# Three of four merge-gate pairs in a Strassen form, interleaved with the branch products of a hybrid decoder layer

## Chip, cores and metric

The kernel runs on one core of one Trainium2 chip. The metric is the device time of one execution in microseconds: 1034.13 us is the median of three runs (1033.95 to 1034.41). TensorE (PE) multiplies, VectorE (DVE) and ScalarE (ACT) work elementwise, GpSimd (POOL) issues some of the transfers, and SyncE (SP) issues the weight loads.

## The reference

One decoder layer for 256 tokens and 2048 channels, all in float32. Its last part is what the change is about:

```python
h = rmsnorm(x, pre_norm_g)
proj = h @ w_in      # ..., g_mla, g_conv (2048 x 2048 each)
attn = causal_mla(...) * silu(z_mla)
y_mla = attn @ w_o_mla
y_conv = (b_gate * conv(c_gate * c_in) * silu(z_conv)) @ w_o_conv
merged = sigmoid(g_mla) * y_mla + sigmoid(g_conv) * y_conv
x = x + rmsnorm(merged @ w_out, post_norm_g)
```

The two merge gates are products of the normed input with 2048 x 2048 weights; so are the two branch outputs and the output projection, each with its own operand.

## The kernel before

**Split products.** Every float32 operand is split into a high part, rounded by ScalarE (`split_act`, L245, `whi`), and the rest, subtracted by VectorE (L246, `wlo`). A product takes three matmuls: high by high, high by low, low by high (`product`). TensorE keeps the order of the program (`matmul`, L88); the other engines run in an order that a scheduler writes when the kernel is built, and each engine works through its own list in that order.

**Units.** Weights come in units of 128 x 2048 float32 (1 MB): four blocks of the contraction by 512 output columns. A unit is loaded by SyncE into one of three `raw` buffers, and split in two halves of 1024 columns, each into one of five `whi` and one of five `wlo` buffers. `ahead` loads three units ahead and splits one ahead of the unit that `take` hands to TensorE. With 256 tokens (two tiles `t` of 128) a unit feeds 2 x 4 x 3 = 24 matmuls of 512 columns: for each token tile the first half, then the second.

**The end of the layer.** After the 16 heads (`at_f` holds the attention branch, `cv_f` the convolution branch) come four column chunks `c` of 512. In each, `tokens(c, n, cols)` makes four blocks: n=0 and n=1 are the two gates (from `x_both`), n=2 the attention branch (`at_both`), n=3 the convolution branch (`cv_both`). A block is four units, 96 matmuls into two PSUM banks named `sq`. Sigmoids by ScalarE make `sg`, VectorE multiplies and adds, the merged chunk is turned through DRAM by GpSimd (`turned`) and split into `m_both` (`features`) while the next chunk's first block runs. In chunk 0 the splits of the branches stand between the units of the first blocks. At the end stands the output projection, `out`.

Unit numbers appear in names: `wlo113` to `wlo116` are the units of block (0, 0), `117` to `120` of block (0, 1).

Of the kernel before, what the change touches and what calls it, by code (L numbers as in the profile page):

```python
# [82 lines left out]
def tile_layer(ctx: ExitStack, tc: tile.TileContext, xw, w0, xb, x, pos, pvec, post_g, wc, wz, wcv, wkr, wqk, wqr, wv, cwr, wsq, out):  # L83
# [55 lines left out]
    u_d = [[[add(wsq[n, c, k]) for k in range(4)] for n in range(4)] for c in range(4)]  # L139
# [28 lines left out]
    def split_unit(i):  # L168
# [22 lines left out]
        for h in range(0, w, HALF):  # L191
            n = min(HALF, w - h)
            if u_out[3, 0] <= i < u_out[3, 3]:
                hi, lo = (op.tile([P, HALF], F32R, name=f"w{o}{i}_{h}") for o in ("hi", "lo"))
# [18 lines left out]
    def take(i):  # L213
        ahead(i)
        parts = splits.pop(i)
# [11 lines left out]
    def product(ps, a, b, first, last):  # L227

        (ah, al), (bh, bl) = a, b
        matmul(ps, ah, bh, start=first, stop=False)  # L230
        matmul(ps, ah, bl, start=False, stop=False)
        matmul(ps, al, bh, start=False, stop=last)
# [51 lines left out]
    hp = main.enter_context(tc.tile_pool(name="hp", bufs=1))  # L284
    x_both = hp.tile([P, KD, 2 * S], F32R, name="x_both")
    fstack = main.enter_context(ExitStack())
# [3 lines left out]
    bstack = main.enter_context(ExitStack())  # L290
# [394 lines left out]
    def values(h, pt):  # L685
# [15 lines left out]
        nc.vector.tensor_tensor(at, f[:, :].rearrange("p (t i x) -> p t i x", t=NT, i=4), at, op=ALU.mult)  # L701


    at_t = at_f[:, :, :].rearrange("p (v t k) s -> p v t (k s)", v=NV, t=NT)
    z_ps = {}
# [56 lines left out]
    def channels_join(j, t):  # L762
# [4 lines left out]
        go, come = turned(u, via, 4)  # L767
        go()
        return lambda: come(u)
# [151 lines left out]
    cp = main.enter_context(tc.tile_pool(name="cp", bufs=1))  # L921
    at_both = cp.tile([P, H, 2 * S], F32R, name="at_both")
    cv_both = cp.tile([P, KD, 2 * S], F32R, name="cv_both")
    dp = main.enter_context(tc.tile_pool(name="dp", bufs=1))

    def split_turned(src, both, c, t):
        ks, ts = slice(4 * c, 4 * c + 4), slice(t * P, (t + 1) * P)
        lo = slice(t * P + S, (t + 1) * P + S)
        split_act(quarters(both[:, ks, ts]), quarters(both[:, ks, lo]), by_rows(src, 4), True)

    def split_branch(i):

        for t in range(NT):
            split_turned(at_t[:, i, t, :], at_both, i, t)

    def split_channels(i):

        j, t = divmod(i, NT)
        split_turned(cv_t[:, j, t, :], cv_both, j, t)

    def tokens(c, n, cols):

        pss = [bank(f"sq{c}_{n}_{t}") for t in range(NT)]
        for kk in range(4):
            w = take(u_d[c][n][kk])
            if c == 0 and n == 0:
                split_branch(kk)
            if c == 0 and n in (1, 2):
                split_channels(4 * (n - 1) + kk)
            for t in range(NT):  # L950
                for k4 in range(4):
                    k = 4 * kk + k4
                    a = [cols[:, k, o + t * P : o + (t + 1) * P] for o in (0, S)]
                    product(pss[t][:, :], a, w(k4, 512), k == 0, k == KD - 1)
        return pss

    def wide(name, t, bufs=1):
        return dp.tile([P, 512], F32, name=f"{name}{t}", tag=f"{name}{t}", bufs=bufs)

    def features(c, m, m_both):  # L960

        for t in range(NT):
            split_turned(m[t][:, :], m_both, c, t)

    make_identity(nc, ident[:, :])
    waiting = m_both = None
    for c in range(4):
        gates = []
        for n in range(2):
# [224 lines left out]
```

## Time and profile before

| | |
|---|---|
| median of three runs (range) | 1034.13 us (1033.95 to 1034.41) |
| span of the profiled execution, first to last instruction | 1032.9 us |
| mean granted TensorE clock | 0.999 |
| chain that ended last | TensorE 99% |
| HBM read, written | 215.66 MB, 12.58 MB |

The profiled execution has no time of its own beside its span; the three runs lie 1.1 to 1.5 us above the span. In the groups, a line has the source line, the engine, the operation, what it writes and reads, shape and count, then busy time and mean duration, then the idle time ahead of it and what ended it. In the timeline, a line begins with start and duration in us, and a wait ahead of the row stands in brackets at its end. A line number may be that of a helper (L88 is every matmul), so one reads by the names of tiles.

### The profile page before, as it was taken

Reading aid. Unit: us, or ns where it says so; the run is one execution under the profiler, and the core shown is the slowest. Engines: PE = TensorE matmul, PEld = TensorE weight load, DVE = VectorE, ACT = ScalarE, POOL = GpSimd, SP = SyncE. Lnnn points to the kernel's source line nnn. Section 1 sums busy time; section 2 is a strip of 40 time slices with the busy share of each in tenths; the row PEclk is TensorE's granted clock in tenths of the full one; section 3 lists DMA queues with packets and bytes.
Section 4 is the critical chain, followed back from the end, with each engine's and each line's share of the span. In section 5 each row is a group of like instructions: output and inputs, shape, how many; then the busy total and the mean of one; then the engine's idle time right before and its main releaser. Section 6 shows DMA issues by size and latency. Waiting matters only on the chain.

```text
span 1032.9 us, 12670 instructions
## 1 busy us (share of the span) xinstructions
PE 1026.4 (99%) x4648; PEld 854.6 (83%) x4648; DVE 687.9 (67%) x973; ACT 531.3 (51%) x750; POOL 174.2 (17%) x324
## 2 busy tenths in 40 slices
PE   9999999999999999999999999999999999999997
PEld 8888888888888888888888888888888888888886
DVE  7588777787687777777777785564455455455562
ACT  7675555655456464564555465344434444443551
POOL 4620421104210223112133120020010001002000
PEclk9999999999999999999999999999999999999999
DMA  9775766558675676857676765565565556558642
GB/s 356 280 257 214 269 215 227 207 191 297 212 252 193 209 279 210 278 184 242 229 271 222 267 217 200 204 222 188 201 218 208 188 202 243 183 187 335 231 165 81
DMA packets 44669, 233.24 MB, mean 226 GB/s; under 512 B 7968, under 2 KB 10656, under 8 KB 21696
## 3 DMA queue, kind: packets, MB, share of 16 engines
q1 hardware_dynamic: 32544, 199.67, 54.4%
q0 software_dynamic: 11632, 29.48, 8.9%
q10 hardware_dynamic: 432, 3.29, 0.8%
q8 instruction: 36, 0.59, 0.2%
q14 instruction: 25, 0.20, 0.1%
HBM read 215.66 MB, written 12.58 MB: 221 GB/s over the span
## 4 chain that ended last, share of the span: by engine, by line
PE 99%; DVE 0%; ACT 0%; issue 0%
PE cv L88 34%; PE sq L88 34%; PE z L88 8%; PE out L88 8%; PE qa L88 2%; PE kn L88 2%; PE qn L88 2%; PE vv L88 2%; PE ckv L88 2%; PE qr L88 1%; PE o L88 1%; PE sw L88 1%; PE sc L88 1%; PE idle L88 0%; PE kr L88 0%; DVE og L1048 0%
## 5 line engine op out<-in xcount | busy, mean ns | idle before, releaser
L246 DVE TENSOR_TENSOR wlo<-raw,whi 128x1024 fp32r<-128x1024 f32 (+1 forms) x370 | 440.5, 1196 | 276.6 <-ACT whi L245 265.5
L245 ACT ACTIVATE whi<-raw 128x1024 fp32r<-128x1024 f32 (+1 forms) x372 | 382.7, 1035 | 412.2 <-PE sq L88 180.5
L88 PE MATMUL cv<-whi,x_both 128*128 128x512 f32 x1024 | 319.8, 389 | 0.0
L88 PEld LDWEIGHTS cv<-whi,x_both 128*128 128x128 f32 x1024 | 192.3, 188 | 39.6
L88 PE MATMUL cv<-wlo,x_both 128*128 128x512 f32 x512 | 199.4, 390 | 0.0
L88 PE MATMUL sq<-whi,x_both 128*128 128x512 f32 x512 | 158.2, 389 | 0.0
L88 PEld LDWEIGHTS sq<-whi,x_both 128*128 128x128 f32 x512 | 96.1, 188 | 19.8
L88 PEld LDWEIGHTS cv<-wlo,x_both 128*128 128x128 f32 x512 | 96.1, 188 | 19.3
L88 PE MATMUL sq<-wlo,x_both 128*128 128x512 f32 x256 | 99.6, 389 | 0.0
L88 PE MATMUL z<-whi,x_both 128*128 128x512 f32 x256 | 80.0, 389 | 0.0
L88 PE MATMUL sq<-whi,at_both 128*128 128x512 f32 x256 | 79.4, 389 | 0.0
L88 PE MATMUL sq<-whi,cv_both 128*128 128x512 f32 x256 | 79.4, 389 | 0.0
L88 PE MATMUL out<-whi,m_both 128*128 128x512 f32 x256 | 79.0, 389 | 0.0
L328 POOL DMA_DIRECT2D far<-sg x32 | 17.5, 553 | 305.8 <-DVE sg L320 232.6
L328 POOL DMA_DIRECT2D far<-via x64 | 35.2, 557 | 191.4 <-DVE via L320 190.0
L88 PEld LDWEIGHTS sq<-wlo,x_both 128*128 128x128 f32 x256 | 48.1, 188 | 10.0
L88 PEld LDWEIGHTS out<-whi,m_both 128*128 128x128 f32 x256 | 48.1, 188 | 10.0
L88 PEld LDWEIGHTS sq<-whi,cv_both 128*128 128x128 f32 x256 | 48.1, 188 | 9.9
L88 PEld LDWEIGHTS sq<-whi,at_both 128*128 128x128 f32 x256 | 48.1, 188 | 9.9
L88 PEld LDWEIGHTS z<-whi,x_both 128*128 128x128 f32 x256 | 48.1, 188 | 9.9
L88 PE MATMUL z<-wlo,x_both 128*128 128x512 f32 x128 | 49.8, 389 | 0.0
L88 PE MATMUL sq<-wlo,at_both 128*128 128x512 f32 x128 | 49.8, 389 | 0.0
(227 smaller groups left out, 1131.3 us busy)
## 6 DMA issues: line engine op xcount, KB each, us to landing
raw<-wsq_dram SPq DMA_DIRECT2D x80, 1024.0 KB, 4.8
raw<-wcv_dram SPq DMA_DIRECT2D x64, 1024.0 KB, 5.5
raw<-wz_dram SPq DMA_DIRECT2D x16, 1024.0 KB, 4.8
raw<-wqk_dram SPq DMA_DIRECT2D x8, 1024.0 KB, 6.1
cw<-cwr_dram POOLq DMA_DIRECT2D x24, 256.0 KB, 5.8
raw<-wc_dram SPq DMA_DIRECT2D x4, 1024.0 KB, 9.8
raw<-wv_dram SPq DMA_DIRECT2D x4, 1024.0 KB, 5.3
far<-via POOLq DMA_DIRECT2D x64, 48.0 KB, 4.1
```

What stands on the lines that cost most here:

```text
L88: return tc.keep_in_program_order(nc.tensor.matmul(*a, **kw))
L245: a = nc.scalar.activation(hi, src, AF.Copy)
L246: b = nc.vector.tensor_tensor(lo, src, hi.bitcast(F32), op=ALU.subtract)
L328: tc.keep_in_program_order(queue.dma_start(out=f[i], in_=m))
```

## The change

Chunk 0 keeps its two plain gate blocks. For chunks 1, 2 and 3 the gate pair is taken as one product of a 2 x 2 block matrix: rows are the two token tiles, columns the two halves of the contraction on the input's side, and the two gates on the weights' side. It is formed with seven products of 128 tokens by 1024 contraction by 512 columns, in the order Q1, V5, V6, V7, V4, V3, Q2, accumulated in three PSUM banks (`sX`, `sZ`, `sY`). A product has two units; a unit feeds 12 matmuls. The seven sums of the input (`form_11` to `form_3`) are made once, beside the gate blocks of chunk 0, from a second copy of x (`xf`). The weight sums are made for each chunk by VectorE in place (`nc.vector.tensor_tensor` on 128 x 2048, L1152 of the new file): V5, V6, V7 and V4 have two each. In names, `slo1_V51_0` is the low part of chunk 1, product V5, unit 1, half 0; `b1_0_2` is the raw unit 2 of gate 0 in chunk 1.

The products of a pair are interleaved with the units of two branch blocks: chunk 1's pair with the attention blocks 0 and 1, chunk 2's with 2 and 3, chunk 3's with the convolution blocks 0 and 1; the convolution blocks 2 and 3 stand by themselves. `at_both` and `cv_both` now share four tiles in the place of `x_both`. The attention and convolution branches, the gates and the half merged chunks are written to DRAM and read back (`keep`, `again`, `turned_unit`). Loads run four units ahead, splits two. The space for descriptors of GpSimd's transfers is set to 4096 bytes.

```diff
-    u_d = [[[add(wsq[n, c, k]) for k in range(4)] for n in range(4)] for c in range(4)]
+    u_d = [[[None] * 4 for n in range(4)] for c in range(4)]
+    for n, c in [(0, 0), (1, 0)] + [(n, c) for n in (2, 3) for c in range(4)]:
+        for k in range(4):
+            u_d[c][n][k] = add(wsq[n, c, k])
...
-        go, come = turned(u, via, 4)
+        go, _ = turned(u, via, 4, far_cv[j][:, 512 * t : 512 * (t + 1)])
         go()
-        return lambda: come(u)
+        return lambda: None
...
+    def keep(key, t):
+        kept[key] = dram.tile([P, 512], F32, name="kept_" + "_".join(map(str, key)))
+        tc.keep_in_program_order(nc.gpsimd.dma_start(out=kept[key][:, :], in_=t[:, :]))
+
+    def again(key, t):
+        tc.keep_in_program_order(nc.gpsimd.dma_start(out=t[:, :], in_=kept[key][:, :]))
...
+    def make_forms():
...
+        for i, h in enumerate(halves):
+            for k in range(KH):
+                nc.vector.scalar_tensor_tensor(
+                    h[:, k, :], h[:, k, :], col("pre_g", KH * i + k), r_x[:, :], op0=ALU.mult, op1=ALU.mult
+                )
+            yield
...
+        form_split("11", a11)
+        u, w, f3, f7 = sums
...
+    def branch_block(c, both):
...
+            early()
+            for t in range(NT):
+                nc.vector.tensor_tensor(y[t][:, :], pss[t][:, :], y[t][:, :], op=ALU.mult)
+                keep(("m", c, t), y[t])
...
+    def paired(c):
...
+        def split(name, src, plus):
+            def go():
+                t = raw[src]
+                if plus:
+                    nc.vector.tensor_tensor(t[:, :], t[:, :], raw[plus][:, :], op=ALU.add)
+                out = []
+                for h in range(2):
+                    hi = wpool.tile([P, HALF], F32R, name=f"shi{c}_{name}_{h}", tag="whi", bufs=5)
+                    lo = wpool.tile([P, HALF], F32R, name=f"slo{c}_{name}_{h}", tag="wlo", bufs=5)
+                    split_act(hi[:, :], lo[:, :], t[:, h * HALF : (h + 1) * HALF])
+                    out.append((hi, lo))
+                return pieces(out)
+            return go
...
+        items = [
+            ("Q1", (0, 0), "rt", None, "11", "X", True, False, lambda: copy("a", "X")),
+            ("V5", (0, 0), None, (1, 0), "5", "Z", True, False, None),
+            ("V6", (0, 0), None, (1, 2), "6", "X", False, False, lambda: copy("b", "X")),
+            ("V7", (1, 0), None, (1, 2), "7", "X", False, False, done_c),
+            ("V4", (0, 0), None, (0, 2), "22", "X", False, True, done_x),
+            ("V3", (1, 2), None, None, "3", "Z", False, True, done_z),
+            ("Q2", (0, 2), None, None, "12", "Y", True, True, done_y),
+        ]
...
+    def interleave(s, p, extra):
+        seq.extend(s["Q1"])
+        seq.extend(extra[:1])
+        seq.extend(s["V5"])
+        seq.extend(extra[1:])
+        for name, n in (("", 1), ("V6", 1), ("V7", 1), ("V4", 2), ("V3", 1), ("Q2", 2)):
+            seq.extend(s.get(name, []))
+            seq.extend(p[:n])
+            del p[:n]
...
+    seq.extend(gate_block(0, 0, "gm", {0: step, 1: step, 2: step, 3: step}))
+    seq.extend(gate_block(0, 1, "gc", {0: step, 1: step}))
...
+    interleave(paired(1), branch_block(0, at_b) + branch_block(1, at_b), at_units)
...
+        while ns < min(j + 3, len(seq)):
+            ready[ns] = seq[ns][1]()
+            ns += 1
```

What moves is best seen on VectorE, which makes the low part of every weight. Before, in the second and third unit of block (0, 1), its list reads:

```order
L246 TENSOR_TENSOR wlo118_0_5742<-raw118_5695,whi118_0_5741 128x1024
L246 TENSOR_TENSOR at_both_5570<-at_f_108,at_both_5570 128x4x128 x8
L246 TENSOR_TENSOR wlo118_1024_5746<-raw118_5695,whi118_1024_5745 128x1024
L246 TENSOR_TENSOR cv_both_5571<-cv_f_109,cv_both_5571 128x4x128
L246 TENSOR_TENSOR wlo119_0_5778<-raw119_5739,whi119_0_5777 128x1024
L246 TENSOR_TENSOR wlo119_1024_5782<-raw119_5739,whi119_1024_5781 128x1024
```

The eight attention splits of 128 x 512 stand together once; after that there is at most one branch split between two units. The new list has them later. From the last split of Q1 in chunk 1 to the first split of V5 it reads:

```order
L253 TENSOR_TENSOR slo1_Q11_1_5898<-b1_0_1_5822,shi1_Q11_1_5897 128x1024
L253 TENSOR_TENSOR at_both0_5939<-turned86_0_5856,at_both0_5939 128x4x128 x2
L253 TENSOR_TENSOR at_both1_5940<-turned86_0_5856,at_both1_5940 128x4x128
L1152 TENSOR_TENSOR b1_0_0_5779<-b1_0_0_5779,b1_1_0_5891 128x2048
L253 TENSOR_TENSOR at_both1_5940<-turned86_0_5856,at_both1_5940 128x4x128
L253 TENSOR_TENSOR at_both2_5941<-turned86_2_5964,at_both2_5941 128x4x128 x2
L253 TENSOR_TENSOR at_both3_5942<-turned86_2_5964,at_both3_5942 128x4x128 x2
L972 TENSOR_TENSOR form_3_5583<-fs1_5593,form_3_5583 128x8x128
L1152 TENSOR_TENSOR b1_0_1_5822<-b1_0_1_5822,b1_1_1_5933 128x2048
L1152 TENSOR_TENSOR b1_1_0_5891<-b1_1_0_5891,b1_1_2_6001 128x2048
L253 TENSOR_TENSOR slo1_V50_0_5969<-b1_0_0_5779,shi1_V50_0_5968 128x1024
```

Branch splits, one form and three weight sums now stand between two splits of weights. A little later, between the two halves of unit 121 (the first unit of attention block 0):

```order
L253 TENSOR_TENSOR slo1_V51_1_5998<-b1_0_1_5822,shi1_V51_1_5997 128x1024
L253 TENSOR_TENSOR wlo121_0_6027<-raw121_5990,whi121_0_6026 128x1024
L1152 TENSOR_TENSOR b1_1_1_5933<-b1_1_1_5933,b1_1_3_6024 128x2048
L1152 TENSOR_TENSOR b1_0_0_5779<-b1_0_0_5779,b1_1_2_6001 128x2048
L1152 TENSOR_TENSOR b1_0_1_5822<-b1_0_1_5822,b1_1_3_6024 128x2048
L253 TENSOR_TENSOR wlo121_1024_6031<-raw121_5990,whi121_1024_6030 128x1024
```

Three more weight sums stand there, ahead of the second half of a unit that TensorE reads in both halves for each token tile. At the change from one chunk to the next, the list before has, in the last block of chunk 0 and the first of chunk 1 (`sg` are the gates):

```order
L246 TENSOR_TENSOR wlo131_0_6235<-raw131_6198,whi131_0_6234 128x1024
L993 TENSOR_TENSOR sg0_1_5735<-sg0_1_5735,sg1_1_5885 128x512
L320 STREAM_TRANSPOSE sg1_1_5885<-sg0_1_5735 128x4x4x32
L246 TENSOR_TENSOR wlo131_1024_6239<-raw131_6198,whi131_1024_6238 128x1024
L246 TENSOR_TENSOR wlo132_0_6269<-raw132_6232,whi132_0_6268 128x1024
L246 TENSOR_TENSOR wlo132_1024_6273<-raw132_6232,whi132_1024_6272 128x1024
L246 TENSOR_TENSOR wlo133_0_6303<-raw133_6266,whi133_0_6302 128x1024
L246 TENSOR_TENSOR wlo133_1024_6307<-raw133_6266,whi133_1024_6306 128x1024
```

The new list has, at the beginning of chunk 2's pair, from the third split of Q1 to the third split of V5 (`y1_0` and `y1_1` are attention chunk 1 by its gate):

```order
L253 TENSOR_TENSOR slo2_Q11_0_6546<-b2_0_1_6430,shi2_Q11_0_6545 128x1024
L1152 TENSOR_TENSOR b2_0_0_6350<-b2_0_0_6350,b2_1_0_6509 128x2048
L1152 TENSOR_TENSOR b2_1_0_6509<-b2_1_0_6509,b2_1_2_6611 128x2048
L253 TENSOR_TENSOR slo2_Q11_1_6550<-b2_0_1_6430,shi2_Q11_1_6549 128x1024
L1110 TENSOR_TENSOR y1_0_6577<-sq125_0_6360,y1_0_6577 128x512
L1110 TENSOR_TENSOR y1_1_6579<-sq125_1_6361,y1_1_6579 128x512
L253 TENSOR_TENSOR slo2_V50_0_6591<-b2_0_0_6350,shi2_V50_0_6590 128x1024
L253 TENSOR_TENSOR slo2_V50_1_6595<-b2_0_0_6350,shi2_V50_1_6594 128x1024
L1152 TENSOR_TENSOR b2_0_1_6430<-b2_0_1_6430,b2_1_1_6543 128x2048
L1152 TENSOR_TENSOR b2_0_0_6350<-b2_0_0_6350,b2_1_2_6611 128x2048
L1152 TENSOR_TENSOR b2_1_1_6543<-b2_1_1_6543,b2_1_3_6636 128x2048
L253 TENSOR_TENSOR slo2_V51_0_6615<-b2_0_1_6430,shi2_V51_0_6614 128x1024
```

Five weight sums and two combinations stand between splits here. Chunk 3's pair has the same order, with four splits of `cv_both` among them.

More of the change, by code (lines that the diff above doesn't have):

```diff
@@ L214, in take, with pieces @@
         ahead(i)
-        parts = splits.pop(i)
+        return pieces(splits.pop(i))
+    def pieces(parts):
         def piece(j, n):
@@ L920, in tile_layer @@
     bstack.close()
[L921 to L949, printed above, removed]
+    fstack.close()
@@ new lines, in tile_layer, with unit, plain, load @@
+    seq = []
+    def unit(load=None, split=None, mm=None, after=None):
+        seq.append([load, split, mm, after])
+    def plain(i, pss, both, kk, after=None):
+        def load():
+            if done["raw"] <= i:
+                load_raw(i)
+                done["raw"] += 1
+        def split():
+            if done["split"] <= i:
+                split_unit(i)
+                done["split"] += 1
+            return pieces(splits.pop(i))
+        def mm(w):
+            if kk == 0:
+                pss.extend(bank(f"sq{i}_{t}") for t in range(NT))
```

321 lines of the change are left out of this document (266 added, 55 removed).

## The prediction

> **What bounds the kernel now.** I read the page first (span, busy time of each engine, the chain that ended last), then that chain in order of time, then one window over the square products, and last the timeline of ScalarE and VectorE at its start.
>
> ```profile
> span 1032.9 us, 12670 instructions
> PE 1026.4 (99%) x4648; PEld 854.6 (83%) x4648; DVE 687.9 (67%) x973; ACT 531.3 (51%) x750; POOL 174.2 (17%) x324
> PE 99%; DVE 0%; ACT 0%; issue 0%
> ...
> 589.95 348.20 PE sq L88 x1536
> 938.15 87.05 PE out L88 x384
> ...
> 589.80:938.00 348.20, 348.20 (x1538) 288.38 (x1538) 192.78 (x190) 156.44 (x168) 22.09 (x41) 1.00 0.58 206
> ```
>
> TensorE is the whole chain. Nearly all that the change touches lies between 589.95 and 938.15 us: 1536 products `sq` with nothing between them, 348.20/1536 = 0.2267 us each, at the full granted clock (the 1.00 in the window's row; before it stand the busy times of PE, PEld, DVE, ACT and POOL). VectorE works 193 of these 348 us, so it has room on the average. What that room is worth depends on how far VectorE can run ahead:
>
> ```profile
> 599.61 1.06 ACT L245 ACTIVATE whi<-raw 128x1024 fp32r<-128x1024 f32 x1 [3.03 <-PE sq L88]
> 600.91 1.07 ACT L245 ACTIVATE whi<-raw 128x1024 fp32r<-128x1024 f32 x1 [0.24 <-PE sq L88]
> ...
> 600.70 2.53 DVE L246 TENSOR_TENSOR wlo<-raw,whi 128x1024 fp32r<-128x1024 f32 x2 [1.23 <-ACT whi L245]
> ...
> 608.59 4.90 DVE L246 TENSOR_TENSOR at_both<-at_f,at_both 128x512 fp32r<-128x512 f32 x8
> ...
> ACT whi L245 <- PE sq L88: 180.5, 110, 3.0
> ```
>
> A half unit (`whi`, `wlo`) has five buffers: half h can be written when TensorE is done with half h-5, and ScalarE waited for that 110 times. The first wait above ends 0.1 us after TensorE leaves the first half of the second unit (589.95 + 5.44 + 4.08 = 599.47). So the lead is five halves and never more. A plain unit is 24 products, 5.44 us; its first half is free after 4.08 us, its second after 5.44, but the second is wanted 1.36 us after the first. Eight splits in a row (608.59) still fit into that lead: the chain shows no gap there.
>
> **Durations.**
>
> ```profile
> L246 DVE TENSOR_TENSOR wlo<-raw,whi 128x1024 fp32r<-128x1024 f32 x352 | 428.3, 1222 | 276.4 <-ACT whi L245 265.3 <-PE qr L88 1.9
> L245 ACT ACTIVATE whi<-raw 128x1024 fp32r<-128x1024 f32 x352 | 370.6, 1059 | 409.4 <-PE sq L88 180.5 <-PE cv L88 126.5 <-PE z L88 31.6
> L246 DVE TENSOR_TENSOR at_both<-at_f,at_both 128x512 fp32r<-128x512 f32 x8 | 4.9, 684 | 0.0
> L351 DVE SCALAR_TENSOR_TENSOR x_both<-raw,pv,x_both 128x256 fp32r<-128x256 f32 x9 | 4.4, 486 | 0.1
> ```
>
> Instructions that follow each other overlap a little: eight of 684 ns take 4.90 us, so one step is (4.90 - 0.68)/7 = 0.60 us, 0.08 less than the duration. By the same 0.08 a step of 128x1024 is 1.14 us and one of 128x256 is 0.40. VectorE's sum of two 128x2048 weights is not in this trace. From 512 to 1024 elements cost 0.538 us, so 2048 elements stream for 2.15 us (lower end); two steps of 1024 make 2.28 (upper end). I take 2.21.
>
> **What TensorE saves.** A gate pair was 2 x 96 products; seven half-depth products are 7 x 24 = 168. Three pairs save 72 products, 72 x 0.2267 = 16.3 us, all on the chain. The Trainium skill (TensorE: Matmul & The Clock Gate, Part 1) gives 215.7 ns from start to start at 512 columns; by it the saving would be 15.5 us. The row decides.
>
> **What VectorE gets.** A Strassen unit feeds only 12 products, 2.72 us, and still needs two splits (2.3 us), and in eight units of fourteen a weight sum too (2.2 us): 4.5 us of VectorE for 2.7 us of TensorE. Over a whole interleave (168 + 192 products, 81.6 us) VectorE has 44 splits (50.2), eight sums (17.7), and up to 8 us of branch splits and combinations: 76 of 81.6 us. It fits on average. But the order puts the work in bursts, and between two splits TensorE can live only on the halves in hand. I count from the first product of each pair (t = 0); its first product, Q1, lasts to 5.44.
>
> - *Pair 1.* VectorE's order is the old one up to 608.59 us. From there it has, up to the last split of Q1, 16 scalings (6.4 us) and 19 steps of 1024 (nine splits, six forms, four sums; 21.7 us): 636.7. TensorE reaches t = 0 at 589.95 + 43.5 = 633.5. With some 0.7 us of waits that split ends at t = 4, just in time; its buffer allows no earlier than -1.36 + 0.1 + 1.06 + 1.22 = 1.0. Then come eight branch splits (4.8), three weight sums (6.6), form_3 and the first split of V5 (2.3): 13.7 us. So V5 begins at 17.7 rather than 5.44: **12.3 us** idle (9.3 by the earlier end). Next, from there to the second half of the following branch unit, stand five splits (5.7) and three sums (6.6), 12.3 us, while TensorE has 5.44 + 1.36 = 6.8: **5.5 us**.
> - *Pair 2.* The third split of Q1 ends at -5.44 + 0.1 + 1.06 + 1.22 = -3.1. Two sums (4.4), a split (1.1), two combinations (1.2), two splits (2.3), three sums (6.6) and the split V51_0 (1.1) follow: 16.7 us, to 13.6. TensorE runs dry at 8.16: **5.4 us**.
> - *Pair 3.* The same with four `cv_both` splits (2.4) in the burst: **7.8 us**.
>
> Sum 31.0 us, and 27 to 35 by the bounds: the earlier end of pair 1 and the shorter sum (16 of them, 0.06 each) below, a hand-over of 1 us more at each of four places above. After each burst VectorE catches up, but the lost time is not given back, since TensorE has no slack anywhere.
>
> **A restart may be slow.** The granted clock falls when TensorE is quiet, and the first products of the run are slow:
>
> ```profile
> 1026.92 1.13 PE L88 MATMUL fin<-og,dg 128*128 128x256 f32 x4 [0.87 <-ACT dg L1070]
> ...
> 1030.00:1031.00 1.00, 0.00 (x0) 0.00 (x0) 0.00 (x0) 0.00 (x0) 0.00 (x0) 0.83 0.94 344
> 1031.00:1032.00 1.00, 0.00 (x0) 0.00 (x0) 0.00 (x0) 0.00 (x0) 0.00 (x0) 0.50 0.01 0
> ...
> 0.77 3.75 PE L88 MATMUL idle<-const-float32-1.0 128*128 128x128 f32 x16 [0.77 <-PEq L1182]
> 4.50 2.08 PE L88 MATMUL qa<-whi,x_both 128*128 128x512 f32 x4
> 6.37 0.76 PE L88 MATMUL qa<-wlo,x_both 128*128 128x512 f32 x2
> 6.97 1.09 PE L88 MATMUL qa<-whi,x_both 128*128 128x512 f32 x4
> ```
>
> The last product ends at 1028.05, and the clock is 0.50 some 2.6 us later. At the start four products take (6.37 - 4.50)/4 = 0.47 us each, twice the later step. Half speed lasts between 1.9 us (those four) and 5.6 us (since the first instruction), so a restart loses 0.9 to 2.8 us; I take 2. In pair 1 it is hidden, since there VectorE sets the pace up to the second stall; in pairs 2 and 3 it counts: **4 us**, 0 to 8. The Trainium skill (same page and part) has half speed after a quiet window of about 3.4 us and full speed after as long a busy one; by it a restart loses an estimated 1.7 to 3.4 us. Here the clock fell after 2.6.
>
> **At nothing.** ScalarE gets 18 more units, 36 casts of 1.06 = 38 us, and seven forms, on 156 of 348 us: it stays behind VectorE. SyncE's second `xf` load waits for GpSimd's last transfers, and the next raw unit is queued behind it; GpSimd's part follows from these rows:
>
> ```profile
> 599.76 2.17 POOL L328 DMA_DIRECT2D far<-mv  x4 [1.26 <-DVE mv L320]
> ...
> raw<-wsq_dram SPq DMA_DIRECT2D x80, 1024.0 KB, 4.8
> far<-sg POOLq DMA_DIRECT2D x32, 64.0 KB, 4.4
> sg<-far POOLq DMA_DIRECT2D x8, 256.0 KB, 5.3
> ```
>
> GpSimd's last issue ends at 601.9, lands by 606, and the `xf` half by 612; it is wanted at about 614.7. If that cover is gone, VectorE is late by as much and so is pair 1. Gates by DRAM: a write (4.4) and a read (5.3) after the gate of Q2 bring `y` back at t = 2.6 in pair 2, where VectorE comes at 2.7; later in a merged block the two `y` buffers make the second row wait about 10 us while VectorE has 9 us of splits, and five halves in hand. I cost it at 0, up to 6 if it slips. GpSimd otherwise works 22 of 348 us, and the DMA share of 0.58 leaves room for some 16 MB more.
>
> **Sum.** 1034.1 (the median; the profiled span is 1.2 us below it, and that difference stays) - 16.3 + 31.0 + 4 = **1052.8 us**. Anything within 0.2% (2 us) I call the same.
>
> **Rivals.**
> - *The lead covers the bursts* (faster): all stalls gone, 1034.1 - 16.3 = 1018, up to 1030 if half of them stay. For it: VectorE's average fits, and eight splits in a row cost nothing before. Against: a Strassen half is 1.36 us of TensorE, so five halves hold at most 6.8 us against bursts of 12 to 14. It decides at 16.3 us of stalls, half of what I sum. Chance 0.10.
> - *The stalls about pay for the saving*: bursts half as long (sums at half the time take 3.3 us from each of four stalls and more in pairs 2 and 3): 1032 to 1036. No row has such a pace. Chance 0.03.
> - *Full clock after a stall*: 1048.8, down to 1045 with the short ends. Chance 0.25.
> - *DRAM round trips late as well* (GpSimd's queue in order, write and read behind each other): 6 to 12 us more, 1060 to 1066. For it: VectorE stands in order behind these reads. Against: the reads are issued early where a buffer is free. Chance 0.17.
> - The forecast, 1049 to 1060 by the bounds of stalls and restarts: 0.45.
>
> Range 1040 to 1066. Faster 0.11 (the first rival and 0.01 of the second), same 0.02 (the rest of the second), slower 0.87.
>
> **What would show it.** After: 1464 `sq`, `sX`, `sZ` and `sY` products in all; TensorE idle before the first `sZ` of pair 1 (over 9 us, released by VectorE's L253 split of V50), before a `sq` of the unit after it, and before V51 in pairs 2 and 3; sums at L1152 near 2.2 us, VectorE busy without a gap through each burst; the granted clock below 1 after them. I am wrong if TensorE idles under 16 us there, if the sums take half that time, or if the idle time stands before products of the merged blocks instead.

## The result, and the profile after

The changed kernel takes 1079.39 us (median of four runs, 1076.04 to 1081.67), the kernel before 1034.27 beside it: a ratio of 1.0431 (95% interval 1.0411 to 1.0450), slower by 45 us where 18.7 were forecast. The profiled execution took 1078.8 us with a span of 1076.8. First the page of the changed kernel (span, busy time of each engine, the chain by engine), then a window over the square products and one over the start of the output projection (busy time and count of PE, PEld, DVE, ACT and POOL, then granted clock, DMA share and GB/s):

```profile
span 1076.8 us, 12835 instructions
PE 1024.1 (95%) x4576; PEld 846.1 (79%) x4576; DVE 802.2 (74%) x1069; ACT 579.4 (54%) x804; POOL 196.9 (18%) x364
PE 85%; DVE 7%; DMA 4%; issue 3%; ACT 1%; POOL 1%; ACTq 0%; DVEq 0%; SPq 0%; POOLq 0%
...
589.50:959.10 369.60, 341.14 (x1465) 278.34 (x1463) 298.43 (x275) 199.76 (x216) 40.18 (x73) 0.96 0.64 233
959.10:1009.30 50.20, 32.62 (x122) 24.93 (x121) 21.27 (x25) 14.36 (x17) 11.05 (x20) 0.86 0.66 237
```

The 72 products are gone (4648 to 4576), and TensorE is 85% of the chain where it was 99%. The square products are 1464 x 0.2267 = 331.9 us of work and took 369.6: **37.7 us lost in the three pairs**. The first 121 products of the output projection are 27.4 us of work and took 50.2: **22.8 us lost in the handover** from the merged blocks (the expectations have 22.7). That closes: 1032.9 - 16.3 + 37.7 + 22.8 = 1077.1 against a span of 1076.8.

In the pairs, TensorE's timeline has the longest waits where they were forecast: in pair 1 ahead of V5's first unit (`sZ`) and in the plain unit behind V5 (`sq`), in pairs 2 and 3 ahead of V5's second unit:

```profile
644.25 0.80 PE L88 MATMUL sZ<-shi_V,form 128*128 128x512 f32 x1 [3.73 <-ACT shi_V L252]
652.79 0.79 PE L88 MATMUL sZ<-slo_V,form 128*128 128x512 f32 x1 [7.74 <-DVE slo_V L253]
665.08 0.50 PE L88 MATMUL sq<-wlo,at_both 128*128 128x512 f32 x1 [3.31 <-DVE wlo L253]
748.40 0.79 PE L88 MATMUL sZ<-slo_V,form 128*128 128x512 f32 x1 [3.89 <-DVE slo_V L253]
839.94 0.79 PE L88 MATMUL sZ<-slo_V,form 128*128 128x512 f32 x1 [3.60 <-DVE slo_V L253]
```

VectorE's timeline at the first of them has no gap; branch splits, weight sums (L1152) and weight splits follow each other. All 24 sums together waited 0.6 us for transfers (last row), so it is not late weights that hold them up:

```profile
642.97 3.09 DVE L253 TENSOR_TENSOR at_both<-turned,at_both 128x512 fp32r<-128x512 f32 x5
645.98 1.22 DVE L972 TENSOR_TENSOR form<-fs,form 128x1024 fp32r<-128x1024 f32 x1
647.12 4.48 DVE L1152 TENSOR_TENSOR b<-b,b 128x2048 f32<-128x2048 f32 x2
651.52 4.62 DVE L253 TENSOR_TENSOR slo_V<-b,shi_V 128x1024 fp32r<-128x1024 f32 x4
656.06 1.22 DVE L253 TENSOR_TENSOR wlo<-raw,whi 128x1024 fp32r<-128x1024 f32 x1
657.20 6.69 DVE L1152 TENSOR_TENSOR b<-b,b 128x2048 f32<-128x2048 f32 x3
...
L1152 DVE TENSOR_TENSOR b<-b,b 128x2048 f32<-128x2048 f32 x24 | 54.3, 2284 | 0.6 <-DMA b<-wsq_dram 0.6
```

In the handover four rows show the longest waits of TensorE, then come GpSimd's list and ScalarE's; the last row is the load of `gb` in the kernel before:

```profile
961.23 0.50 PE L88 MATMUL out<-whi,m_both 128*128 128x512 f32 x1 [2.12 <-ACT whi L252]
977.68 0.80 PE L88 MATMUL out<-whi,m_both 128*128 128x512 f32 x1 [4.21 <-ACT whi L252]
981.47 0.79 PE L88 MATMUL out<-wlo,m_both 128*128 128x512 f32 x1 [2.99 <-DVE wlo L253]
994.29 0.80 PE L88 MATMUL out<-wlo,m_both 128*128 128x512 f32 x1 [5.71 <-DVE wlo L253]
...
959.94 2.20 POOL L336 DMA_DIRECT2D far_m<-vg  x4 [5.55 <-DVE vg L328]
971.80 0.57 POOL L1064 DMA_DIRECT2D turned<-far_m  x1 [9.66 <-DMA raw<-wsq_dram]
972.36 0.57 POOL L960 DMA_DIRECT2D vg<-kept_gc  x1
980.60 2.21 POOL L336 DMA_DIRECT2D far_m<-vg  x4 [6.60 <-DVE vg L328]
982.80 0.57 POOL L960 DMA_DIRECT2D vg<-kept_gc  x1
...
959.19 0.34 ACTq L1357 DMA_DIRECT2D gb<-post_g_dram  x1
959.56 0.46 ACTq L1358 DMA_DIRECT2D xr<-x_dram  x1
960.12 3.90 ACT L252 ACTIVATE whi<-raw 128x1024 fp32r<-128x1024 f32 x4 [12.15 <-DVE vg L328]
...
938.19 0.33 ACTq L1023 DMA_DIRECT2D gb<-post_g_dram  x1
```

GpSimd issues the gate reads of block 3's first half (`vg`, 972.36) only behind the read back of merged chunk 2 (971.80), and those of the second half (982.80) only behind the write of the first (980.60), which waits for VectorE, which waits for the read: one round trip after the other. ScalarE, idle for 12.15 us, has the loads of `gb` and `xr` at the head of its list; they go into the space that `cv_both` leaves when block 3 ends. That order of events does not say which of these costs what; the experiments do.

### The profile page after: what moved, and what is told of

The parts are those of the page before. It is cut to its first block, busy times and chain, and to the rows that moved or that the text cites. A ratio compares the mean times of both kernels' runs of the same rounds, so it can differ in the third digit from the quotient of the medians.

```text
span 1076.8 us, 12835 instructions
## 1 busy us (share of the span) xinstructions
PE 1024.1 (95%) x4576; PEld 846.1 (79%) x4576; DVE 802.2 (74%) x1069; ACT 579.4 (54%) x804; POOL 196.9 (18%) x364
## 4 chain that ended last, share of the span: by engine, by line
PE 85%; DVE 7%; DMA 4%; issue 3%; ACT 1%; POOL 1%; ACTq 0%; DVEq 0%; SPq 0%; POOLq 0%
PE cv L88 32%; PE sq L88 16%; PE z L88 8%; PE out L88 6%; PE sX L88 5%; PE sZ L88 2%; PE kn L88 2%; PE qa L88 2%; PE qn L88 2%; PE vv L88 2%; PE ckv L88 2%; PE sY L88 2%; DVE b L1152 1%; DVE wlo L253 1%; PE qr L88 1%
## 5 line engine op out<-in xcount | busy, mean ns | idle before, releaser
L252 ACT ACTIVATE whi<-raw 128x1024 fp32r<-128x1024 f32 (+1 forms) x318 | 324.2, 1031 | 274.5 <-PE cv L88 126.5
L253 DVE TENSOR_TENSOR wlo<-raw,whi 128x1024 fp32r<-128x1024 f32 (+1 forms) x316 | 371.4, 1190 | 128.2 <-ACT whi L252 119.6
L252 ACT ACTIVATE shi_V<-b 128x1024 fp32r<-128x1024 f32 x60 | 62.3, 1056 | 75.4 <-DVE b L1152 37.1
L253 DVE TENSOR_TENSOR slo_V<-b,shi_V 128x1024 fp32r<-128x1024 f32 x60 | 72.4, 1222 | 24.7 <-ACT shi_V L252 23.4
L88 PE MATMUL sq<-whi,cv_both 128*128 128x512 f32 x256 | 79.8, 389 | 0.0
L88 PE MATMUL out<-whi,m_both 128*128 128x512 f32 x208 | 67.6, 403 | 7.4 <-ACT whi L252 7.4
L1152 DVE TENSOR_TENSOR b<-b,b 128x2048 f32<-128x2048 f32 x24 | 54.3, 2284 | 0.6 <-DMA b<-wsq_dram 0.6
L88 PEld LDWEIGHTS out<-whi,m_both 128*128 128x128 f32 x208 | 40.7, 196 | 17.1 <-ACT whi L252 8.6
L88 PE MATMUL out<-wlo,m_both 128*128 128x512 f32 x104 | 42.4, 407 | 10.2 <-DVE wlo L253 10.2
L88 PE MATMUL sq<-wlo,cv_both 128*128 128x512 f32 x128 | 49.8, 389 | 0.0
```

The costliest lines, as they stand in the source:

```text
L88: return tc.keep_in_program_order(nc.tensor.matmul(*a, **kw))
L252: a = nc.scalar.activation(hi, src, AF.Copy)
L253: b = nc.vector.tensor_tensor(lo, src, hi.bitcast(F32), op=ALU.subtract)
L1152: nc.vector.tensor_tensor(t[:, :], t[:, :], raw[plus][:, :], op=ALU.add)
```

## The experiments

Theory 1: the sums of weights on VectorE make the loss in the pairs. Theory 2: the handover is lost to the order of lists (GpSimd's reads, ScalarE's two loads, the slots for merged chunks). Rivals stand in the expectations. The kernel before lay between 1034.1 and 1034.6 beside all of them.

| run | edit | median us | ratio to before (95%) |
|---|---|---|---|
| e1 | changed kernel, no sums | 1043.11 | 1.0078 (1.0061 to 1.0095) |
| e2 | sums and V splits in program order | 1096.13 | 1.0595 (1.0567 to 1.0623) |
| e3 | merged chunks into other tiles | 1076.46 | 1.0406 (1.0390 to 1.0423) |
| e4 | gb, xr later, by GpSimd | 1073.59 | 1.0387 (1.0366 to 1.0408) |
| e15 | gate reads early | 1064.21 | 1.0296 (1.0279 to 1.0314) |
| e16 | e3 and e15 | 1065.93 | 1.0302 (1.0287 to 1.0318) |
| e5 | e3, e4 and e15 | 1057.78 | 1.0225 (1.0210 to 1.0240) |
| e6 | e5, sums by GpSimd | 1110.70 | 1.0738 (1.0722 to 1.0754) |
| e7 | e5, sums by transfers | 1089.62 | 1.0537 (1.0519 to 1.0554) |
| e8 | e5, plain units moved | 1049.22 | 1.0147 (1.0129 to 1.0166) |
| e9 | e8, V7's sums by transfers | 1048.23 | 1.0137 (1.0118 to 1.0155) |
| e10 | e8, a plain unit ahead of V5 | 1044.58 | 1.0099 (1.0084 to 1.0114) |
| e11 | e10, some of VectorE's order kept | 1037.57 | 1.0028 (1.0018 to 1.0039) |
| e12 | e11 and two edits | 1040.10 | 1.0056 (1.0042 to 1.0070) |
| e13 | e11, gates of block 2 not by DRAM | 1032.45 | 0.9979 (0.9970 to 0.9988) |
| e14 | e13, two plain units ahead in pair 1 | 1033.68 | 0.9988 (0.9979 to 0.9996) |

**e1, without the sums.**

```diff
-                if plus:
+                if plus and False:
```

> The 24 sums of weight tiles are left out (each Strassen split reads the unsummed tile, so the output is not the reference's); everything else stays as in the changed kernel. Theory 1 (VectorE's sums, standing in bunches ahead of the weight splits, make the 37.7 us that the three pairs lose): 24 x 2.2 = 53 us leave VectorE's list, what stays is the branch splits and gate products, a few us; the pairs lose at most 10 us, the output stage still loses its 22.7 us, so 1079.4 - 28 to 35 = 1044 to 1052 us. Rival (the loss in the pairs comes from something else: the split lead as such, transfers, the clock): the pairs still lose over 25 us, time above 1066 us.

Measured 1043.11 us, 36.3 us less and 0.9 below theory 1's range. Of the pairs' waits, three stay in pair 1 (1.5 + 1.9 + 1.8 us) and none in pairs 2 and 3, as windows of this run over them show:

```profile
740.00:760.00 20.00, 20.00 (x90) 16.57 (x89) 14.48 (x13) 12.83 (x15) 0.54 (x1) 1.00 0.69 247
820.00:860.00 40.00, 40.00 (x178) 33.14 (x177) 28.27 (x25) 24.96 (x26) 3.82 (x7) 1.00 0.53 191
```

Theory 1 holds. In the handover TensorE still waits 12.2 us, where it waited 17.6 in the changed kernel, so the two losses are separate for the most part.

**e2, the sums in the order of the program.**

```diff
-                    nc.vector.tensor_tensor(t[:, :], t[:, :], raw[plus][:, :], op=ALU.add)
+                    tc.keep_in_program_order(
+                        nc.vector.tensor_tensor(t[:, :], t[:, :], raw[plus][:, :], op=ALU.add)
+                    )
...
-                    split_act(hi[:, :], lo[:, :], t[:, h * HALF : (h + 1) * HALF])
+                    split_act(hi[:, :], lo[:, :], t[:, h * HALF : (h + 1) * HALF], later=True)
```

> The 24 sums and the low parts of the Strassen splits keep the order in which the program writes them: each sum stands right ahead of its own unit's splits, none ahead of an earlier unit's. No work is added or removed. Theory 1 in its form 'bunching' (it is the order and not the load): the gaps of 7.7, 3.7 and 3.3 us in pair 1 and the 3.9 and 3.6 us ones in pairs 2 and 3 go for the most part; the pairs lose 8 to 16 us in place of 37.7, so 1079.4 - 22 to 30 = 1050 to 1058 us. Rival 'load' (a V half pair and a plain unit take 11.3 us of VectorE against 10.9 us of TensorE, so the loss comes whatever the order): 1072 to 1080 us.

Both missed: 1096.13 us, 17 us worse. VectorE's timeline of this run shows what is new:

```profile
657.79 2.29 DVE L1153 TENSOR_TENSOR b<-b,b 128x2048 f32<-128x2048 f32 x1
661.29 2.36 DVE L253 TENSOR_TENSOR slo_V<-b,shi_V 128x1024 fp32r<-128x1024 f32 x2 [1.21 <-ACT shi_V L252]
663.57 2.29 DVE L1153 TENSOR_TENSOR b<-b,b 128x2048 f32<-128x2048 f32 x1
667.06 2.36 DVE L253 TENSOR_TENSOR slo_V<-b,shi_V 128x1024 fp32r<-128x1024 f32 x2 [1.20 <-ACT shi_V L252]
```

With each sum right ahead of its own split, VectorE waits 1.2 us for ScalarE's high part behind every sum. A sum that stands early fills such a wait; so early is not wrong as such, only ahead of a split that TensorE is already waiting for. That these waits make the whole 17 us is not shown.

**e3, e4, e15, e16, e5: the handover.** e3:

```diff
-            t = wpool.tile([P, UNIT], F32, name=f"turned{len(seq)}_{first}", tag="raw", bufs=3)
+            if queue is nc.gpsimd:
+                t = sum_tile(f"turned_m{first}", ("rt", "rb", "rc")[first % 3])
+            else:
+                t = wpool.tile([P, UNIT], F32, name=f"turned{len(seq)}_{first}", tag="raw", bufs=3)
```

> The four chunks of the merged values are read back into the tiles of the Strassen weights (free after pair 3), not into slots of the three weight tiles; all else stays. Theory 2b (on GpSimd's queue the read of chunk 2 waits 9.7 us for a weight slot, and the gate reads of block 3 stand behind it; VectorE and ScalarE wait 10 to 15 us for these): the waits of GpSimd for a slot go, the gaps of 4.2, 3.0 and 5.7 us in the output stage and the half-speed products behind them go: 14 to 20 us of the 22.7, so 1060 to 1066 us. Rival 2a (ScalarE's loads of gb and xr hold its list) : under 5 us, 1074 us or more.

e4:

```diff
-    nc.scalar.dma_start(out=gb[:, :], in_=post_g.to_broadcast([P, D]))
-    nc.scalar.dma_start(out=xr[:, :, :], in_=x)
+    tc.keep_in_program_order(nc.gpsimd.dma_start(out=gb[:, :], in_=post_g.to_broadcast([P, D])))
+    tc.keep_in_program_order(nc.gpsimd.dma_start(out=xr[:, :, :], in_=x))
```

> The loads of gb and xr are issued by GpSimd behind its last read of merged values, not by ScalarE behind the end of the last merged block; all else stays. Theory 2a (ScalarE's list stands from 948 to 960 because these two loads wait for the space of cv_both): ScalarE splits block out's weights as they land, the gaps of 2.1, 0.8 us at 961 go and with them a part of those at 977 to 994: 5 to 12 us, so 1067 to 1074 us. Rival 2b: only the first two gaps and the slow products behind them go, 3 to 4 us, 1075 to 1076 us, the later ones stay.

Measured 2.9 us (e3) and 5.8 us (e4) less: theory 2a within its range, 2b refuted; a free slot did not help, since the reads behind it still came one after the other. e5 has both and this (behind units 0 and 2 of block 2; `reads[c]` issues the reads of both halves, block 3's `vg` and `vm` into tiles of their own):

```diff
+    for c, v in ((2, b2[0]), (3, b2[2])):
+        old_r = v[3]
+        v[3] = lambda old_r=old_r, c=c: (reads[c](), old_r and old_r())
```

> Three edits to the stage around the start of the output projection, the pairs unchanged: the merged chunks are read back into the Strassen weights' tiles (as in the third run), gb and xr are loaded behind them by GpSimd (as in the fourth), and the gates and branch products that merged blocks 2 and 3 read are all issued at the start of block 2, block 3's into tiles of their own, so that no read stands on GpSimd's queue behind a write that waits for VectorE. Theory 2c (the order of GpSimd's queue: the reads of block 3 came one half after the other, each behind the write of the half before): the output stage loses 3 to 6 us in place of 22.7, so 1079.4 - 17 to 20 = 1059 to 1063 us. Rival 2d (the round trip of a merged chunk is itself too long: write, completion and read back take over 20 us whatever stands ahead): 1069 to 1074 us, with the gap before the products of the last chunk.

1057.78 us, 21.6 us less (1.2 below 2c's range), with no wait of TensorE left in this stage. GpSimd's timeline of e5 has all six reads of block 3 issued by 942, ahead of the writes:

```profile
939.36 0.55 POOL L960 DMA_DIRECT2D vg<-kept_gc  x1
941.34 0.55 POOL L960 DMA_DIRECT2D vg<-kept_gc  x1
...
958.71 2.18 POOL L336 DMA_DIRECT2D far_m<-vg  x4 [1.92 <-DVE vg L328]
```

Three edits at once do not say which one did it, so two more:

> Only the third edit of the fifth run: the gates and branch products of merged blocks 2 and 3 are read at the start of block 2; the merged chunks still come back into slots of the weight tiles, gb and xr are still loaded by ScalarE. Theory 2c alone (the reads behind waiting writes on GpSimd's queue are the whole loss of the output stage): 16 us or more below the changed kernel's 1079.4, 1058 to 1064 us. Theory 'all three' (the read back of chunk 2 still waits for a weight slot, and ScalarE's list still stands behind gb and xr): 6 to 13 us below, 1066 to 1073 us.

> The first and third edit of the fifth run: reads early and merged chunks into other tiles; gb and xr are still loaded by ScalarE. If the ScalarE loads alone hold the weights' high parts as in the changed kernel (idle 948 to 960): 3 to 6 us above the fifth run, 1061 to 1064 us. If the loads only waited because the raw slots and the block's end were late: within 1.5 us of the fifth run, 1056 to 1059 us.

The reads alone bring 15.2 us (e15), a little short of the 16 that 2c alone expects and more than its rival's 13. With the other tiles added nothing more comes (e16, 1.7 us above e15), and the loads of `gb` and `xr` then cost 8.2 us over e5, more than either expectation had. How they cost it changed: in e16 they no longer stand ahead of the high parts in ScalarE's list, but their 3 MB run beside the weights. Windows of e16 (first two rows) and of e5 (the next two) over the same stretch, and the piece of e16's chain in it:

```profile
965.00:970.00 5.00, 5.00 (x24) 4.14 (x23) 2.51 (x3) 2.12 (x2) 2.19 (x4) 1.00 1.03 432
970.00:975.00 5.00, 1.86 (x9) 1.20 (x7) 1.23 (x1) 1.23 (x2) 0.00 (x0) 1.00 1.00 421
...
965.00:970.00 5.00, 5.00 (x24) 4.14 (x23) 3.21 (x5) 2.72 (x5) 0.55 (x1) 1.00 0.74 261
970.00:975.00 5.00, 5.00 (x24) 4.14 (x23) 2.04 (x2) 1.98 (x2) 1.66 (x3) 1.00 0.75 259
...
962.01 12.72 DMA raw<-wsq_dram
```

The transfer engines are full (1.00 to 1.03) and a weight of the output projection takes 12.72 us. In the kernel before they are as full behind the same two loads (1.03 from 943 to 948), and TensorE does not wait; why the lead of the weights covers it there and not in e16 stays open. So the handover's loss is about 15 us for the order of the reads and 6 to 8 us for the two loads.

**e6, e7: the sums off VectorE**, on top of e5, with `nc.gpsimd.tensor_tensor` in e6, and in e7:

```diff
-                    nc.vector.tensor_tensor(t[:, :], t[:, :], raw[plus][:, :], op=ALU.add)
+                    nc.gpsimd.dma_start(out=t[:, :], in_=wsq[plus[0], c, plus[1]], accum_op=ALU.add)
```

> The run before it, and the 24 sums of weight tiles done by GpSimd in place of VectorE. Theory 1 (the load of the sums on VectorE makes the loss of the pairs): if a sum takes GpSimd under 6 us and VectorE is not slowed by it, the pairs lose 5 to 15 us in place of 37.7: 22 to 33 us below the run before, 1028 to 1040 us. Rival (GpSimd takes over 8 us for one, so that 8 sums of a pair, 64 us and more of the 85 us of a pair, come too late one after the other, or VectorE's splits get longer while GpSimd sums): no gain or a loss, 1060 us or more.

> The run before the last, and the 24 sums of weight tiles done by accumulating transfers: the second tile is read from HBM once more and added on the way into the first. VectorE and GpSimd do nothing for them but the issue; 25 MB more are moved in 255 us. Theory 1: the pairs lose 5 to 15 us, 22 to 33 us below the run with the handover mended, 1028 to 1040 us. Rival (an accumulating transfer is slow, over 15 us for 1 MB, or takes the 16 queues from the weights): the splits wait for transfers in place of VectorE, 1055 us or more.

Both came out at the rivals' times, 53 and 32 us worse than e5. Of the conditions one came true, the longer splits of VectorE in e6; a sum took GpSimd less than 8 us, and an accumulating transfer less than 15. Of e6 the group of sums and the durations (min/median/max in ns) of V's low parts on VectorE, of e7 the group of V's high parts and the two kinds of transfer (KB, median us from issue to landing):

```profile
L1172 POOL TENSOR_TENSOR b<-b,b 128x2048 f32<-128x2048 f32 x24 | 126.0, 5258 | 69.6 <-DMA b<-wsq_dram 33.9 <-DVE slo_V L253 23.4 <-DVE slo_Q L253 5.3
L253 DVE TENSOR_TENSOR slo_V<-b,shi_V x60: 1208/1226/10077, 651.2 to 945.2; 128x1024 fp32r<-128x1024 f32 x60
```

```profile
L252 ACT ACTIVATE shi_V<-b 128x1024 fp32r<-128x1024 f32 x60 | 62.1, 1055 | 111.2 <-DMA b<-wsq_dram 79.8 <-PE sq L88 29.5 <-PE sX L88 1.8
b<-wsq_dram SPq DMA_DIRECT2D x24, 1024.0 KB, 7.4
b<-wsq_dram POOLq DMA_DIRECT2D x24, 1024.0 KB, 11.9
```

A sum takes GpSimd 5.26 us in the mean, and some of VectorE's splits, still 1.23 us in the median, take up to 10.1. By transfer the sums are late: ScalarE waits 79.8 us for transfers into their tiles. A sum in place can only be issued when the splits that read the tile are done, and GpSimd waited 76.6 us for V's low parts ahead of these issues.

**e8, e9: where the plain units stand.** e8:

```diff
-        for name, n in (("", 1), ("V6", 1), ("V7", 1), ("V4", 2), ("V3", 1), ("Q2", 2)):
+        for name, n in (("", 2), ("V6", 2), ("V7", 2), ("V4", 1), ("V3", 0), ("Q2", 1)):
```

> The handover mended (the fifth run), and in each pair two plain units stand behind V5, V6 and V7, one behind V4, none behind V3 and one behind Q2 (before: 1, 1, 1, 2, 1, 2). The work is the same. A V product with two sums needs 4.4 + 4.9 = 9.3 us of VectorE against 5.4 us of TensorE, a plain unit 2.4 against 5.4: with one plain unit between them VectorE has 11.7 us in 10.9, with two 14.1 us in 16.3. Theory 1 (VectorE's load in the stretch from V5 to V4 decides): the later waits in the pairs go, the first one at each V5 (sums of V7 and V6 stand ahead of V5's splits there) stays: 5 to 12 us below the fifth run, 1046 to 1053 us. Rival (only the bunch ahead of V5 costs, which this edit doesn't touch): 1055 to 1060 us.

> The run before it, and the two sums of V7 in each pair done by accumulating transfers (6 in all, 11.9 us each where all 24 were done so), issued as soon as V5's sum has read the tile; V7 comes 25 us and more later. VectorE is relieved of 6 x 2.2 = 13.2 us, and these sums no longer stand ahead of V5's low parts. Theory 1: the waits of TensorE at V5 in each pair shrink by up to the 4.4 us of these two sums and the restarts with them, 8 to 15 us below the run before it: 1034 to 1042 us. Rival (the accumulating transfers delay the weights, or V5 waits for its own sums whatever stands beside them): within 3 us of the run before it.

e8 took 8.6 us off, as theory 1 has it. e9 brought 1.0 us, within the interval. TensorE's wait of 5.54 us at V5 in pair 1 is the same in both, so it was not V7's sums that made it. In pair 2 the waits did shrink, from 5.3 to 1.7 us, but in pair 3 one of 5.25 us came up: there VectorE waits 5.30 us, with V5's next splits behind it, for gates of block 2 that GpSimd reads back between its accumulating transfers.

**e10 to e14.** e10 puts one of the plain units ahead of V5. e11 keeps an order on VectorE: the low parts of V5, then those of the branch's second half, then those of V6, then V7's sums.

```diff
         seq.extend(extra[:1])
+        seq.extend(p[:1])
+        del p[:1]
         seq.extend(s["V5"])
...
+                    if name[:2] == "V7":
+                        tc.keep_in_program_order(add)
...
-                    split_act(hi[:, :], lo[:, :], t[:, h * HALF : (h + 1) * HALF])
+                    split_act(hi[:, :], lo[:, :], t[:, h * HALF : (h + 1) * HALF], later=name[:2] in ("V5", "V6"))
...
```

> The eighth run with one plain unit moved from behind V5 to ahead of it (1 ahead of V5, then 1, 2, 2, 1, 0, 1); the sums are placed as they come. Theory 1 (what is left are the bunches ahead of V5: 4.4 us of its own sums, the branch splits and the sums of V7 stand on VectorE in the 5.4 us that Q1 lasts on TensorE): 10.9 us in place of 5.4 to do them in; the gaps at V5 of 0.8 + 2.9 + 1.7 (pair 2) and 2.2 + 1.1 (pair 3) go, that of 5.5 in pair 1 shrinks: 6 to 11 us below the eighth run's 1049.2, 1038 to 1043 us. Rival (the chain sum, high part, low part of V5 is late because its tiles arrive late): 1047 to 1050 us, V5 then waits behind the plain unit.

> The run before it, and three groups keep their order on VectorE: the low parts of V5 and V6, behind V5's those of the second half of the branch (at_both, cv_both 2 and 3), and behind V6's the two sums of V7, which so no longer stand ahead of V5's or V6's splits. Nothing is added or removed. Theory 1: the rest of the waits at V5 and V6 goes but for 5 to 8 us in pair 1, where the forms of x are still made: 3 to 7 us below the run before it, 1032 to 1038 us. Rival (what an order kept by hand gains ahead of V5 it loses at V7, as in the second run): no lower than the run before it.

Both came out in the direction of theory 1: e10 took 4.6 us off where 6 to 11 were expected, e11 7.0 us, the upper end. A wait of another kind is new in e10's pair 3, 5.38 us; in e11 2.96 us of it were left:

```profile
817.28 0.77 PE L88 MATMUL sq<-whi,cv_both 128*128 128x512 f32 x1 [2.96 <-DVE y L1113]
```

Merged block 0 needs the PSUM bank of branch block 2, whose product with its gates (`y`) needs these to go to DRAM and come back. GpSimd issues their reads at 811.65, and VectorE, which has no gap here, makes the product at 816.45, behind other work; with the edit below it makes it at 808.50.

The edit of e13, which e12 has too (`gates` is the pair's table of gate tiles, for block 2 alone):

```diff
-            early()
+            if gates:
+                y.extend(wide(f"y{c}_{t}", "y", 2) for t in range(NT))
+            else:
+                early()
             for t in range(NT):
-                nc.vector.tensor_tensor(y[t][:, :], pss[t][:, :], y[t][:, :], op=ALU.mult)
+                g = gates["ad"[t]] if gates else y[t]
+                nc.vector.tensor_tensor(y[t][:, :], pss[t][:, :], g[:, :], op=ALU.mult)
...
-            keep((key, c, t), g)
+            if c != 2 or key != "gm":
+                keep((key, c, t), g)
```

> The eleventh run with two edits. First, the gates of branch block 2 are multiplied from the tiles in which they are made, not sent to DRAM and read back (in the eleventh run this product came late and held the PSUM bank that merged block 0 needs: TensorE waited 2.96 us there in pair 3). Second, the low parts of the plain unit ahead of V5 and both sums of V5 keep their order on VectorE, the low parts first (a sum stood ahead of them, and TensorE waited 4.09 us for them in pair 1). Theory 1 and 2 together (what is left are waits for things that stand in the wrong order, no lack of VectorE): the 2.96 + 0.97 us of pair 3 and some 2 us of pair 1 go, with 1 us of slow products behind each: 1030 to 1034 us, a little under the kernel before. Rival (VectorE is full from 620 to 660, so that what the plain unit gains V5 loses): pair 3's part alone, 1033 to 1036 us.

> The eleventh run and only the first edit of the twelfth: the gates of branch block 2 are multiplied from the tiles in which they are made, not sent to DRAM and read back. If the DRAM route of these gates holds the PSUM bank that merged block 0 needs in pair 3: the eleventh run's 2.95 us wait there and the 1 us behind it go, with a restart of the clock: 1037.6 - 4 to 5.5 = 1032 to 1034 us. Rival (another thing is late behind it, the splits of pair 3 as in the twelfth run): 1036 to 1038 us.

> The run before it, and in pair 1 two plain units ahead of V5 in place of one (2 ahead of V5, then 1, 1, 2, 1, 0, 1). Theory 'order': 16.3 us of TensorE's work in place of 10.9 lie over VectorE's forms, branch splits and sums there; the waits of 1.3 + 4.1 + 2.0 us in pair 1 shrink to some 4: 2 to 4 us below the run before it, 1028 to 1032 us. Theory 'load' (VectorE has no free time from 620 to 660, so that the sum of TensorE's waits in pair 1 is set by its work): within 1.5 us of the run before it.

e12 missed, at 1040.10: its second edit, the plain unit's low parts ahead of both sums of V5, cost 7.6 us against e13, which has the first edit alone. e13 takes **1032.45 us** and lies 0.21% (0.12 to 0.30) below the kernel before and 47 us below the changed one. e14 is 1.2 us above it: theory "load". In the windows from 640 to 660, of e13 and then of e14, VectorE is busy 20.00 and 19.00 of 20 us and TensorE 13.97 and 15.93; e14 only moves the wait, to 666 and 689.

```profile
640.00:660.00 20.00, 13.97 (x53) 10.73 (x52) 20.00 (x18) 9.23 (x10) 0.00 (x0) 0.90 0.76 297
640.00:660.00 20.00, 15.93 (x60) 12.59 (x60) 19.00 (x16) 9.11 (x12) 0.00 (x0) 0.83 0.79 297
```

e13's span is 1030.3 against 1016.6 without any loss: 13.7 us of the 16.3 are still paid, most of it in pair 1, where the seven sums of x, the branch splits and the weight sums all fall between 620 and 680.

## Why the prediction was wrong

The direction was right, and so was the mechanism in the pairs. The time lay 13 us above the range, and one stage made that: without the 22.8 us of the handover it would have been 1056.6. Two steps of the prediction failed there. The round trips of the gates by DRAM stood "at nothing", and the loads of `gb` and `xr` in no term. With the first of them mended alone the time falls back into the range (e15, 1064.21).

- *The saving*, 16.3 us: right; the accounts above close with it to 0.3 us.
- *The stalls in the pairs with their restarts*: forecast 31.0 + 4 = 35.0, measured 37.7, of which TensorE was idle for 28.5 (369.60 - 341.14) and lost 9.2 to slow products. By pair: 17.8 forecast and 19.9 measured, 7.4 and 7.6, 9.8 and 10.2. The `xf` load, named as a cover that could go, made VectorE wait 2.82 us ahead of pair 1 (first row below). So the last split of Q1 ended at 639.05 (second row), 6.1 us behind the pair's first product (632.96) where 4 were forecast; the 13.7 us of VectorE's work that were counted from there lead to 652.75, and TensorE went on at 652.79. That is the 2.1 us of pair 1. The slow products of pair 1, 3.5 us, lie under VectorE's pace, as forecast. e1 shows the cause of most of the loss, the sums: without them TensorE waits 5.2 us in the pairs.

```profile
611.04 3.26 DVE L990 SCALAR_TENSOR_TENSOR xf<-xf,pv,r_x 128x256 f32<-128x256 f32 x8 [2.82 <-DMA xf<-xf_dram]
637.83 1.22 DVE L253 TENSOR_TENSOR slo_Q<-b,shi_Q 128x1024 fp32r<-128x1024 f32 x1
```

- *The sum of two weights*: taken at 2.21 us a step; (6.69 - 2.28)/2 = 2.20 measured.
- *A restart*: taken at 2 us; the granted clock after the 7.74 us wait was 0.50 for 3.9 us (rows at the end), which loses 2.
- *"At nothing", gates by DRAM*: this step failed. It was put at 0, up to 6, for merged blocks with two `y` buffers and "five halves in hand"; the order of these reads cost 15.2 us (e15). The working was done for the merged blocks inside pair 3, where Strassen units lie over the reads. Blocks 2 and 3 stand alone, with single buffers, and behind them comes a stage that needs their results. When block 3 ends, at 959.1, both of its halves are still to be read (972.36 and 982.80, 10.4 us apart), and the last merged chunk has to be written and read back behind them, against 27.4 us of TensorE's other work.
- *The loads of `gb` and `xr`* were in no term at all. Both kernels issue them when the last square product ends (938.19 and 959.19). In the kernel before they held nothing up: the next high part started at 942.27, released by TensorE. In the changed one four high parts stand behind them in ScalarE's list, and their 3 MB run beside the weights: 6 to 8 us (e5 against e15 and e16; e4 alone 5.8).
- *The rival "DRAM round trips late as well"* named the mechanism (GpSimd's queue in order, write and read behind each other) with 6 to 12 us at a chance of 0.17. "The reads are issued early where a buffer is free" spoke against it; in blocks 2 and 3 no buffer was free and the reads stood behind writes.
- *The rival "the lead covers the bursts"* fell, as forecast. What makes the lead cover more, plain units between the bursts and another order on VectorE, is worth 25.3 us by the runs from e5 to e13, the gates of block 2 included.
- *The signs of being wrong* all looked at the pairs, the sums and the merged blocks, and none came true: the handover's idle time stands before products of `out`.
- *Two sums of the rivals* are off: half of the stalls would give 1033 us, not 1030, and 6 to 12 us more than the forecast are 1059 to 1065 us, not 1060 to 1066. Neither decides anything here.

## What to carry to other kernels

When a change sends values through DRAM, follow the queue that issues the transfers instruction by instruction to the point where their result is needed, above all in the last block, where no later work lies over it; a read queued behind a write that waits for that read's neighbour makes a chain of round trips. Where a helper engine is nearly full in a stretch, count what it does between two deadlines of the main engine, and first move the main engine's cheap work between them: that brought 13.2 us here (e8, e10), while moving the helper's work to GpSimd or to transfers made it worse. Loads that only follow a buffer's release belong behind the loads that are waited for.

## What the runs showed of the hardware

A sum of two 128x2048 float32 tiles took GpSimd 5.26 us in the mean (4.49 at the least) where VectorE takes 2.28, and beside it single low parts on VectorE took up to 10.1 us while their median stayed at 1.23: they are blocked, not slowed. The longest began at 752.72, 0.04 us behind two sums of GpSimd that follow each other (752.68 to 761.71), and ended 1.1 us after the second. The Trainium skill (SBUF — State Buffer, Who interferes with whom) says this of a VectorE operation on two SBUF inputs beside a GpSimd one that reads SBUF: the second fully blocks until the first is done; e6 agrees. An accumulating transfer of 1 MB landed 11.9 us after its issue where a plain one took 7.4. The granted clock of the changed kernel around the restart at 652.79, in windows of 1 us (clock third from the end), was 0.50 until about 656.7 and then full:

```profile
653.00:654.00 1.00, 1.00 (x3) 0.81 (x4) 1.00 (x2) 0.00 (x0) 0.00 (x0) 0.50 0.18 74
656.00:657.00 1.00, 1.00 (x4) 0.79 (x3) 1.00 (x2) 0.39 (x1) 0.00 (x0) 0.62 0.00 0
657.00:658.00 1.00, 1.00 (x6) 0.80 (x5) 1.00 (x2) 0.00 (x0) 0.00 (x0) 1.00 0.00 0
```
